# Second feed-forward product of a hybrid layer as one level of Strassen's scheme, on one Trainium2 core

## The chip, the cores and the metric

One core of a Trainium2 chip runs the whole kernel. TensorE (PE) does matrix products, VectorE (DVE) and ScalarE (ACT) elementwise work, GpSimd (POOL) a little set-up, and SyncE (SP) issues most DMAs. The metric is the device time of one execution in microseconds, the median of several.

## The reference

One layer of a model with 512 tokens (L), width 1024 (D) and a feed-forward width of 4096 (FF); everything is fp32. After a mixing part with attention comes the end that matters here:

```python
merged = jax.nn.sigmoid(gate_a) * ya + jax.nn.sigmoid(gate_b) * yb
y = merged @ w_out[l]
x = x + ga1 * rmsnorm(y, g_post_mix[l])

h = rmsnorm(x, g_pre_ffn[l]) * (1.0 + sc2) + sh2
u = jax.nn.relu(h @ w_ff1[l])
y = (u * u) @ w_ff2[l]
x = x + ga2 * rmsnorm(y, g_post_ffn[l])
```

Here ya and yb are the outputs of the two mixers times their `up` weights, gate_b is made late as h times the `gate` weights, and ga1, sc2, sh2 and ga2 are columns of silu(c) @ w_ada.

## The kernel before

Every fp32 product is made of three matmuls in a reduced fp32 format: an operand is split into a high half (a copy rounded to that format, on ScalarE, L109) and a low half (the difference, on VectorE, L110), and high x high, high x low and low x high are added up in PSUM (mm3, L137 through mm). A weight block of 128 x 1024 (512 KB) comes by `stage` (L103 to L106): one DMA on SyncE's queue into one of three buffers of the ring `st`, handed out in program order. `wload` (L115 to L125) splits it into `whi` and `wlo`, four buffers each, and a fifth where the list `wmore` names a pool.

The stages in order: attention with the first projections; the merge stage (L629 to L676), which for each of eight column blocks m has 24 matmuls of a `gate` block (on `hTh`, `hTl`, into `mm`) and 24 of an `up` block (on `obh`, `oah` and their low halves, into `s`), and some columns of the product of `ada` with silu(c), made on VectorE (L210) from `in_ada_dram` blocks in the same ring; the product with `w_out` (L704 to L783), with the norm of each token tile behind it, which leaves `h2h` and `h2l`; the first feed-forward product (L786 to L813); the second (L814 to L846).

silu_rows (L154 to L160) makes silu(c) as rows: a DMA `cb` of c to all 128 partitions, a sigmoid into `sg` (tile name `cs`), and a product. It is called twice, at the merge stage and in front of the first feed-forward product. The vector products that follow in each stage read `cb`.

The first feed-forward product takes its first four weights (EARLY) in two halves, tiles 0 and 1 and then tiles 2 and 3. Work on the engines is put in order by a scheduler from the program and its dependencies; buffers of a ring are taken in program order.

The second product goes over 32 blocks k of the 4096 rows. For each it splits u[k] (uh, ul) and the weight block, and for four token tiles t adds 3 x 2 matmuls of 128 x 512 into eight PSUM banks (accs): 768 matmuls. The last four blocks (LAST) are taken tile by tile, so that the norm, gate and store of one tile (residual) run beside the matmuls of the next.

Of the kernel before, what the change touches and what calls it, by code (L numbers as in the profile page):

```python
# [14 lines left out]
P = 128  # L15
# [23 lines left out]
LAST = 4  # L39
# [22 lines left out]
def layer_kernel(tc, x, ada, vecs, c_row, rope, w_first, w_v, w_b, w_a, w_gate, w_up, w_out, w_ff1, w_ff2, out):  # L62
    nc = tc.nc
    es = ExitStack()
    with es:
# [631 lines left out]
        wmore.append(x1p)  # L697
# [92 lines left out]
        silu_rows(f2p)  # L790

        def ff1(m, w, t0, t1):
# [21 lines left out]
        accs = [[bank(a), bank(b)] for a, b in (("tr", "tr"), ("mm", "mm"), ("s", "s"), ("s", "o"))]  # L814

        def ff2(t, k, uw, ns):
            (uh, ul), (hi, lo) = uw
            ts = slice(t * P, (t + 1) * P)
            f, l = k == 0, k == MF - 1
            for s, w, first, last in ((uh, hi, f, False), (uh, lo, False, False), (ul, hi, False, l)):  # L820
                for n in ns:
                    mm(accs[t][n], s[:, ts], w[:, n * 512:(n + 1) * 512], first, last)

        def operands(k):
            w = wload(w_ff2[k])
            uh = f2p.tile([P, L], F32R, name=uid("uh"), tag="uh", bufs=5)
            ul = f2p.tile([P, L], F32R, name=uid("ul"), tag="ul", bufs=5)
            split(uh, ul, u2[k])
            return (uh, ul), w
# [5 lines left out]
        uws = [operands(k) for k in range(MF - LAST, MF)]  # L835
        ov = out.rearrange("(t p) d -> t p d", p=P)
        for t in range(NT):
            for n in range(2):
                for i in range(LAST):
                    ff2(t, MF - LAST + i, uws[i], (n,))  # L840
# [78 lines left out]
```

## Time and profile before

| | us |
|---|---|
| median of 3 runs | 811.65 (811.42 to 813.32) |
| profiled execution | 811.92 |
| its span | 810.1 |
| TensorE busy | 786.3 (97%) |
| VectorE busy | 511.0 (63%) |
| ScalarE busy | 363.0 (45%) |
| attention ends (last `o` matmul) | 324.55 |
| first `w_ff1` matmul | 452.20 |
| first and last matmul of the second product | 629.5, 803.6 |

The profile is one execution, recorded by the hardware; times in it are microseconds from the start of its span. Engines run at the same time, so that only work on the chain that ends last counts. Matmuls overlap one another in the engine: one of 512 columns is listed with some 389 ns, while they start 0.227 us apart. The times of DMA issues are when SyncE's queue gave them out; a DMA lands some microseconds later.

### The profile page before, as it was taken

How to read it: one execution, taken by the hardware profiler on the slowest of the kernel's cores; microseconds unless marked ns; L12 is line 12 of the kernel's file. 1: busy time of each engine (PE TensorE's matmuls, PEld its weight loads, DVE VectorE, ACT ScalarE, POOL GpSimd, SP SyncE). 2: the span in 40 equal slices, each digit the busy share in tenths (PEclk: the TensorE clock that was granted, in tenths of full speed). 3: DMA queues.
4: the chain of work that ended last, by engine and by line, in shares of the span. 5: the costliest groups of instructions: out<-in, count | busy, mean ns of one | idle time of the engine just before them, and what ended most of it. 6: DMA issues, size and time to landing. Idle time of an engine off the chain costs nothing.

```text
span 810.1 us, 10809 instructions
## 1 busy us (share of the span) xinstructions
PE 786.3 (97%) x4110; PEld 656.4 (81%) x4110; DVE 511.0 (63%) x973; ACT 363.0 (45%) x684; POOL 2.8 (0%) x15
## 2 busy tenths in 40 slices
PE   6999999989999999999999999999999999999996
PEld 5889977658889887887688998888888888888885
DVE  6876799999956776788767863344433433333325
ACT  6555657464546677631347753223322322332322
POOL 0000000000000000000000000000000000000000
PEclk9999999999999999999999999999999999999999
DMA  9933201122121210578780332344442232233202
GB/s 356 377 117 104 78 27 53 56 75 79 60 98 53 79 53 27 163 264 256 248 315 28 123 127 89 131 138 137 141 156 99 83 105 89 93 104 104 79 1 104
DMA packets 27987, 98.58 MB, mean 122 GB/s; under 512 B 3360, under 2 KB 3360, under 8 KB 27936
## 3 DMA queue, kind: packets, MB, share of 16 engines
q1 hardware_dynamic: 27216, 96.82, 35.2%
q10 hardware_dynamic: 720, 1.08, 0.4%
q8 instruction: 32, 0.52, 0.3%
q14 instruction: 19, 0.16, 0.1%
HBM read 95.79 MB, written 2.10 MB: 121 GB/s over the span
## 4 chain that ended last, share of the span: by engine, by line
PE 76%; DVE 15%; DMA 6%; issue 2%; ACT 2%; DVEq 0%; SPq 0%; ACTq 0%
PE mm L137 30%; PE s L137 27%; PE o L137 9%; PE tr L137 7%; DMA st<-in_ada_dram 3%; DVE a L483 3%; DVE isc L409 2%; DVE sm L408 2%; DVE wlo L110 2%; DMA st<-in_w_up_dram 2%; PE tr L427 1%; DVE be L485 1%; DVE st L210 1%; PE tr L333 1%; DVE qT L521 1%
## 5 line engine op out<-in xcount | busy, mean ns | idle before, releaser
L109 ACT ACTIVATE whi<-st 128x1024 fp32r<-128x1024 f32 (+2 forms) x122 | 127.5, 1047 | 180.8 <-PE mm L137 45.3
L110 DVE TENSOR_TENSOR wlo<-st,whi 128x1024 fp32r<-128x1024 f32 (+2 forms) x122 | 147.1, 1209 | 92.2 <-ACT whi L109 91.9
L137 PE MATMUL mm<-hTh,whi 128*128 128x512 f32 x192 | 78.7, 410 | 0.1
L110 DVE TENSOR_TENSOR ul<-u,uh 128x512 fp32r<-128x512 f32 x32 | 22.2, 692 | 89.7 <-ACT uh L109 89.6
L137 PE MATMUL mm<-hTh,wlo 128*128 128x512 f32 x192 | 75.6, 394 | 0.0
L137 PE MATMUL mm<-hTl,whi 128*128 128x512 f32 x192 | 75.4, 393 | 0.0
L109 ACT ACTIVATE uh<-u 128x512 fp32r<-128x512 f32 x32 | 20.2, 631 | 108.7 <-PE o L137 105.1
L137 PE MATMUL mm<-whi,hTh 128*128 128x256 f32 (+2 forms) x208 | 62.3, 306 | 0.1
L137 PE MATMUL mm<-whi,hTl 128*128 128x256 f32 (+2 forms) x208 | 60.2, 296 | 0.0
L137 PE MATMUL mm<-wlo,hTh 128*128 128x256 f32 (+2 forms) x208 | 60.1, 295 | 0.0
L210 DVE CUSTOM_DVE_ANT_0 st<-st,cb,vec 128x1024 f32<-128x1024 f32 x32 | 40.9, 1282 | 29.1 <-DMA st<-in_ada_dram 29.0
L137 PE MATMUL s<-h2h,whi 128*128 128x512 f32 (+1 forms) x144 | 52.7, 366 | 0.0
L137 PE MATMUL s<-h2l,whi 128*128 128x512 f32 (+1 forms) x144 | 52.6, 366 | 0.0
L137 PE MATMUL s<-h2h,wlo 128*128 128x512 f32 (+1 forms) x144 | 52.6, 366 | 0.0
L137 PEld LDWEIGHTS mm<-hTh,wlo 128*128 128x128 f32 x192 | 36.3, 189 | 7.8
L137 PEld LDWEIGHTS mm<-hTh,whi 128*128 128x128 f32 x192 | 36.5, 190 | 6.6 <-DVE qT L521 0.3
L137 PEld LDWEIGHTS mm<-hTl,whi 128*128 128x128 f32 x192 | 36.5, 190 | 6.2
L137 PEld LDWEIGHTS mm<-wlo,hTh 128*128 128x128 f32 x208 | 39.5, 190 | 1.0
L137 PEld LDWEIGHTS mm<-whi,hTl 128*128 128x128 f32 x208 | 39.5, 190 | 0.6
L137 PEld LDWEIGHTS mm<-whi,hTh 128*128 128x128 f32 x208 | 39.0, 190 | 0.7 <-ACT ka L544 0.3
L137 PE MATMUL mm<-h2h,wlo 128*128 128x512 f32 (+1 forms) x96 | 35.7, 372 | 0.0
L137 PE MATMUL mm<-h2h,whi 128*128 128x512 f32 (+1 forms) x96 | 35.7, 371 | 0.0
(296 smaller groups left out, 1755.1 us busy)
## 6 DMA issues: line engine op xcount, KB each, us to landing
st<-in_w_ff_dram SPq DMA_DIRECT2D x64, 512.0 KB, 3.3
st<-in_ada_dram SPq DMA_DIRECT2D x32, 512.0 KB, 4.2
sa<-in_ada_dram SPq DMA_DIRECT2D x16, 512.0 KB, 8.1
st<-in_w_gate_dram SPq DMA_DIRECT2D x16, 512.0 KB, 3.3
st<-in_w_first_dram SPq DMA_DIRECT2D x8, 512.0 KB, 8.5
st<-in_w_b_dram SPq DMA_DIRECT2D x8, 512.0 KB, 3.3
st<-in_w_a_dram SPq DMA_DIRECT2D x8, 512.0 KB, 3.2
st<-in_w_up_dram SPq DMA_DIRECT2D x8, 512.0 KB, 4.3
```

The costliest lines, as they stand in the source:

```text
L109: nc.scalar.activation(dst_hi, src, AF.Copy)
L110: nc.vector.tensor_tensor(dst_lo, src, dst_hi.bitcast(F32), op=ALU.subtract)
L137: nc.tensor.matmul(o, lhsT, rhs, start=start, stop=stop)
L210: nc.vector.tensor_tensor_reduce(out=st, in0=st, in1=cb[0], scale=1.0, scalar=vec[:, j:j + 1], op0=ALU.mult, op1=ALU.add, accum_out=mod[:, ...
L333: nc.tensor.transpose(ps[:, t * P:(t + 1) * P], s[:, t, i:i + 2].rearrange("p a d -> p (a d)"), identr)
L408: nc.vector.max(out=m8, in_=cur)
L409: nc.vector.match_replace(out=cur, in_to_replace=m8, in_values=cur, imm_value=SENT)
L427: nc.tensor.transpose(tr[:, j * P:(j + 1) * P], ps[e][:, j * P:(j + 1) * P], ident)
L483: nc.vector.tensor_tensor_scan(a[:, n - 1::-1], a[:, n - 1::-1], zero.to_broadcast([P, n]), 1.0, op0=ALU.mult, op1=ALU.add)
L485: nc.vector.tensor_tensor(be[:, :n - 1], be[:, :n - 1], a[:, 1:n], op=ALU.mult)
L521: nc.vector.scalar_tensor_tensor(qq[o, e], ps[r], QK_SCALE, qq[r, e].bitcast(F32), op0=ALU.mult, op1=ALU.subtract)
```

## The change

The second feed-forward product becomes one level of Strassen's scheme in the form with seven products: the tokens, the 4096 rows and the 1024 output columns are each cut in two halves. Blocks of u are paired (p = 0 to 15, two blocks of 128 rows). A first pass over the pairs makes four of the seven block products (p1, p5, p6, p7), each a half of the tokens by a half of the columns, 24 matmuls of 512 columns a step; then their sums are formed in PSUM and SBUF (u2, c22, v7), and a second pass adds the three others (18 matmuls a step) onto p1, p5 and p7. The sums of u (token_sums) are made behind the first product, the sums of weights in front of each step: the right halves of both weight blocks of a pair come as a new argument, w_right, and from step 2 on the difference to the block that was loaded is made by a DMA of GpSimd that adds w_right onto the negated copy (column_sums). In this part the order on TensorE, VectorE and ScalarE is written out by hand (manual_schedule). LAST is 3.

Two more edits stand in the diff. silu_rows takes `sg` from the ring `st` in place of its own tile, and the fifth weight buffer (wmore) is dropped.

```diff
...
-LAST = 4
+LAST = 3
+NP = MF // 2
+HB = L // 2
+A11, S1, S3, S2, A12, A22 = range(6)
...
         def silu_rows(pool):
             dst = pool.tile([P, D], F32, name=uid("cb"), tag="cb")
-            sg = pool.tile([P, D], F32, name=uid("cs"), tag="cs")
+            sg = per.tile([P, D], F32, name=uid("cs"), tag="st", bufs=3)
             nc.sync.dma_start(dst, c_row.to_broadcast([P, D]))
             nc.scalar.activation(sg, dst, AF.Sigmoid)
             nc.vector.tensor_tensor(dst, dst, sg, op=ALU.mult)
...
-        wmore.append(x1p)
...
-        u2 = [u2p.tile([P, L], F32, name=f"u2_{m}") for m in range(MF)]
+
+        def block_tile(name, dt):
+            return u2p.tile([P, 6 * HB], dt, name=uid(name), tag="ub", bufs=NP)
+
+        blocks = [block_tile("ub", F32) for p in range(NP)]
         f2p = es.enter_context(tc.tile_pool(name="f2p", bufs=1, side="right"))
         ga2b = f2p.tile([P, D], F32, name="ga2b")
         silu_rows(f2p)
...
+            u = blk(m // 2, 4 * (m % 2), 2)[:, cs]
+            nc.scalar.activation(u, ps[:, cs], AF.Relu)
+            nc.vector.tensor_tensor(u, u, u, op=ALU.mult)
+
+        def token_sums(p):
+            nc.vector.tensor_tensor(blk(p, S3), blk(p, A11), blk(p, S1), op=ALU.subtract)
+            nc.vector.tensor_tensor(blk(p, S1), blk(p, S1), blk(p, A22), op=ALU.add)
+            nc.vector.tensor_tensor(blk(p, S2), blk(p, S1), blk(p, A11), op=ALU.subtract)
...
         for m in range(EARLY, MF):
             ff1(m, wload(w_ff1[m]), 0, NT)
-            if m % 2 and m >= MF - 2 * KT:
-                i = (m - MF + 2 * KT) // 2
-                ada_cols(40 + i)
-                gated_gain(KT + i, 40 + i, 72 + i)
+            if m % 2:
+                token_sums(m // 2)
+                if m >= MF - 2 * KT:
+                    i = (m - MF + 2 * KT) // 2
+                    ada_cols(40 + i)
+                    gated_gain(KT + i, 40 + i, 72 + i)
         rows_of(ga2b, ga[:, KT:], evac)
...
-        for k in range(MF - LAST):
-            uw = operands(k)
-            for t in range(NT):
-                ff2(t, k, uw, (0, 1))
...
+        p1, p6, p5, p7 = [[bank(a), bank(b)] for a, b in (("tr", "tr"), ("s", "o"), ("s", "s"), ("mm", "mm"))]
...
+        def load(j):
+            xw[j] = stage(w_ff2[2 * j]) if j < NP else stage(w_ff2[2 * (j - NP) + 1])
+
+        def column_sums(p):
+            nw[p] = ntile().bitcast(F32)
+            nc.scalar.activation(nw[p], xw[p], AF.Copy, scale=-1.0)
+            nc.gpsimd.dma_start(nw[p], w_right[p], accum_op=ALU.add)
+
+        def first_ops(p):
+            a = pair_tile(p, "ah")
+            x, n = xw[p], nw[p]
+            (h1, l1), (h2, l2) = wtile(), wtile()
+            t2 = blk(p, 0, 2)
+            if p != 1:
+                split(a[:, 0], a[:, 1], blk(p, 0, 4))
+            split(h1[:, H0], l1[:, H0], x[:, H0])
+            if p < 2:
+                nc.vector.tensor_tensor(n, n, x, op=ALU.subtract)
+            if p == 1:
+                split(h2, l2, n)
+                split(a[:, 0], a[:, 1], blk(p, 0, 4))
+            nc.vector.tensor_tensor(t2, n[:, H1], x[:, H0], op=ALU.add)
+            if p != 1:
+                split(h2, l2, n)
+            split(h1[:, H1], l1[:, H1], t2)
+            nc.vector.tensor_tensor(blk(p, S2), blk(p, A12), blk(p, S2), op=ALU.subtract)
+            firsts[p] = (a[:, 0], a[:, 1]), (h1, l1), (h2, l2)
+
+        def first_products(p):
+            a, w1, w2 = firsts.pop(p)
+            order = [(p1, A11, w1, H0), (p5, S1, w2, H0), (p7, S3, w2, H1), (p6, S2, w1, H1)]
+            if p in (0, NP - 1):
+                order = [order[i] for i in ((0, 1, 3, 2) if p == 0 else (0, 3, 1, 2))]
+            for acc, b, w, cs in order:
+                for i in range(2):
+                    product(acc, i, a, b * HB, w, cs, p == 0, p == NP - 1)
...
+        def second_ops(p):
+            if p:
+                a = block_tile("a2", F32R)
+                ah, al = a[:, :3 * HB], a[:, 3 * HB:]
+            else:
+                a = pair_tile(0, "ah")
+                ah, al = a[:, 0, :3 * HB], a[:, 1, :3 * HB]
+            y, n, w = xw[NP + p], ntile(), wtile()
+            t2 = blk(p, 0, 2)
+            split(w[0], w[1], y)
+            nc.vector.tensor_tensor(t2, y[:, H0], t2, op=ALU.subtract)
+            split(ah, al, blk(p, 3, 3))
+            split(n[:, H0], n[:, H1], t2)
+            seconds[p] = (ah, al), w, (n[:, H0], n[:, H1])
...
+        on_p1, on_p5, on_p7 = (p1, 1, 1, H0), (p5, 0, 1, H1), (p7, 2, 2, H0)
+
+        for j in range(2):
+            load(j)
+            if j == 0:
+                nw[0] = stage(w_right[0])
+        first_ops(0)
+        nw[1] = stage(w_right[1])
+        load(2)
+        for p in range(NP):
+            if p + 1 < NP:
+                first_ops(p + 1)
+                if p == 0:
+                    load(3)
+                    column_sums(2)
+            if p == NP - 1:
+                second_ops(0)
+            load(p + 4)
+            if p + 3 < NP:
+                column_sums(p + 3)
+            first_products(p)
+        u2 = f3p.tile([P, 2, 512], F32, name="u2")
+        c22 = f3p.tile([P, 2, 512], F32, name="c22")
+        v7 = f2p.tile([P, D], F32, name="v7", tag="cb")
+        for i in range(2):
+            nc.scalar.activation(u2[:, i], p1[i], AF.Copy)
+        for i in range(2):
+            nc.vector.tensor_tensor(u2[:, i], p6[i], u2[:, i], op=ALU.add)
+        for i in range(2):
+            nc.scalar.activation(c22[:, i], p5[i], AF.Copy)
+        for i in range(2):
+            nc.scalar.activation(v7[:, i * 512:(i + 1) * 512], p7[i], AF.Copy)
+        second_ops(1)
+        for p in range(NP - LAST):
+            load(NP + p + 4) if p + 4 < NP else None
+            second_ops(p + 2)
+            for args in (on_p1, on_p5, on_p7):
+                for i in range(2):
+                    second_product(*args, p, i)
...
```

The diff leaves out the operands of each step (first_ops, second_ops make the splits that the program's matmuls read), the change-over between the passes, and the new loop over the last steps, which takes the tiles in the order 2, 3, 0, 1. In both kernels the names of a tile in the following rows end in numbers that the program gives out; lines of the changed kernel stand two or three later. The rows of the trace write `in_w_ff_dram` for the weights of both feed-forward products.

SyncE's queue at the end of the attention, before. `st` from `in_w_up_dram`, `in_w_gate_dram` and `in_ada_dram` are the merge stage's weights, `cb` is silu_rows' first load:

```order
L105 DMA st_618_3199<-in_w_gate_dram 128x1024
L105 DMA st_733_3628<-in_w_up_dram 128x1024
L105 DMA st_737_3660<-in_w_gate_dram 128x1024
L105 DMA st_742_3698<-in_w_up_dram 128x1024
L105 DMA st_746_3730<-in_w_gate_dram 128x1024
L105 DMA st_751_3768<-in_ada_dram 128x1024
L105 DMA st_752_3772<-in_ada_dram 128x1024
L105 DMA st_753_3776<-in_ada_dram 128x1024
L157 DMA cb_730_3620<-in_c_row_dram 128x1024
L105 DMA st_754_3780<-in_w_up_dram 128x1024
```

The same stretch of SyncE's queue in the changed kernel:

```order
L108 DMA st_618_3199<-in_w_gate_dram 128x1024
L160 DMA cb_730_3620<-in_c_row_dram 128x1024
L108 DMA st_733_3628<-in_w_up_dram 128x1024
L108 DMA st_737_3660<-in_w_gate_dram 128x1024
L108 DMA st_742_3698<-in_w_up_dram 128x1024
L108 DMA st_746_3730<-in_w_gate_dram 128x1024
L108 DMA st_751_3768<-in_ada_dram 128x1024
L108 DMA st_752_3772<-in_ada_dram 128x1024
L108 DMA st_753_3776<-in_ada_dram 128x1024
L108 DMA st_754_3780<-in_w_up_dram 128x1024
```

`cb` moved from behind seven weight loads to a place ahead of them. On TensorE the blocks that use the first of these weights stood, in part, ahead of the attention's last matmuls (`o`); before:

```order
L137 MATMUL s_741_3667<-obh_727_3609,wlo_735_3631 128x512
L137 MATMUL s_740_3666<-oah_589_3085,whi_734_3630 128x512
L427 MATMUL tr_724_3570<-identr_69,p_720_3548 128x128 x4
L137 MATMUL o_725_3577<-pT_680_3432,va_79_589 64x512
L137 MATMUL o_725_3577<-pT_681_3433,va_79_589 64x512
L137 MATMUL o_725_3577<-pT_680_3432,va_79_589 64x384
```

and in the changed kernel the last four of the attention are followed by the first of the `up` block:

```order
L140 MATMUL o_725_3577<-pT_681_3433,va_79_589 64x256
L140 MATMUL o_725_3577<-pT_680_3432,va_79_589 64x128
L140 MATMUL o_725_3577<-pT_681_3433,va_79_589 64x128
L140 MATMUL s_741_3667<-obh_726_3608,whi_734_3630 128x512
L140 MATMUL s_741_3667<-obl_728_3610,whi_734_3630 128x512
```

Thirteen matmuls of that `up` block and thirteen of a `gate` block stood ahead of the last `o` matmul; all 26 stand behind it now.

SyncE's queue at the start of the first feed-forward product, before:

```order
L717 DMA x1_3_4284<-in_x_dram 128x1024
L105 DMA st_914_4802<-in_w_ff1_dram 128x1024
L105 DMA st_917_4808<-in_w_ff1_dram 128x1024
L105 DMA st_920_4814<-in_w_ff1_dram 128x1024
L105 DMA st_923_4820<-in_w_ff1_dram 128x1024
L105 DMA st_934_5042<-in_w_ff1_dram 128x1024
L105 DMA st_938_5075<-in_w_ff1_dram 128x1024
L105 DMA st_942_5108<-in_w_ff1_dram 128x1024
L105 DMA st_946_5141<-in_w_ff1_dram 128x1024
L157 DMA cb_912_4797<-in_c_row_dram 128x1024
L105 DMA st_950_5174<-in_w_ff1_dram 128x1024
```

and in the changed kernel:

```order
L108 DMA st_843_4342<-in_w_out_dram 128x1024
L160 DMA cb_928_4781<-in_c_row_dram 128x1024
L108 DMA st_930_4786<-in_w_ff1_dram 128x1024
L108 DMA st_933_4792<-in_w_ff1_dram 128x1024
L108 DMA st_936_4798<-in_w_ff1_dram 128x1024
```

`cb` stood behind eight `w_ff1` loads and now stands ahead of the first.

## Rows read from the trace of the kernel before

**Rows 1.** The page, part 1: busy time (share of the span) x instructions.

```profile
PE 786.3 (97%) x4110; PEld 656.4 (81%) x4110; DVE 511.0 (63%) x973; ACT 363.0 (45%) x684; POOL 2.8 (0%) x15
```

**Rows 2.** Stretches: width, then PE, PEld, DVE, ACT, POOL busy, clock, DMA share, GB/s.

```profile
6.00:8.00 2.00, 0.04 (x1) 0.07 (x1) 0.98 (x3) 1.94 (x6) 0.00 (x0) 1.00 1.00 395
330.00:405.00 75.00, 72.14 (x312) 57.66 (x312) 62.30 (x102) 23.01 (x31) 0.00 (x0) 1.00 0.76 244
629.00:804.00 175.00, 175.00 (x775) 144.44 (x773) 64.36 (x78) 50.88 (x74) 0.00 (x0) 1.00 0.25 85
806.00:808.00 2.00, 0.00 (x0) 0.00 (x0) 1.04 (x2) 0.00 (x0) 0.00 (x0) 0.76 0.36 139
808.00:810.00 2.00, 0.00 (x0) 0.00 (x0) 0.00 (x0) 0.00 (x0) 0.00 (x0) 0.50 0.32 123
```

**Rows 3.** Matmuls by form, 620 to 810: count, ns min/median/max, first to last start.

```profile
L137 PE MATMUL mm<-whi,uh x64: 387/389/474, 629.5 to 792.3; 128*128 128x512 f32 x64
...
L137 PE MATMUL o<-whi,uh x32: 389/389/389, 634.1 to 803.2; 128*128 128x512 f32 x32
```

**Rows 4.** The chain of waits, 324 to 405: shares by engine and line.

```profile
by line: DMA st<-in_ada_dram 28.4%; DMA st<-in_w_up_dram 16.2%; PE s L137 13.3%; DVE st L210 12.3%; DVE wlo L110 7.5%; DMA st<-in_w_gate_dram 5.5%; ACT whi L109 5.3%; issue 3.7%; PE mm L137 3.1%; DVE mrg L662 1.7%; PE o L137 0.9%; DVE mrg L
```

**Rows 5.** SyncE's issues around the attention's end: start, us, what.

```profile
253.41 0.33 SPq L105 DMA_DIRECT2D st<-in_w_up_dram  x1
...
324.62 0.33 SPq L157 DMA_DIRECT2D cb<-in_c_row_dram  x1
332.48 0.33 SPq L105 DMA_DIRECT2D st<-in_w_up_dram  x1
```

**Rows 6.** SyncE's issues at the start of the first feed-forward product.

```profile
416.66 41.52 SPq L105 DMA_DIRECT2D st<-in_w_ff_dram  x8
463.69 0.33 SPq L157 DMA_DIRECT2D cb<-in_c_row_dram  x1
```

**Rows 7.** Groups by form, 629.4 to 804: count, busy us, mean ns, idle before.

```profile
L110 DVE TENSOR_TENSOR wlo<-st,whi 128x1024 fp32r<-128x1024 f32 x28 | 34.3, 1225 | 6.9 <-ACT whi L109 6.9
...
L109 ACT ACTIVATE whi<-st 128x1024 fp32r<-128x1024 f32 x28 | 29.2, 1044 | 3.9 <-PE mm L137 3.9
...
L110 DVE TENSOR_TENSOR ul<-u,uh 128x512 fp32r<-128x512 f32 x27 | 18.7, 693 | 88.2 <-ACT uh L109 88.2
L109 ACT ACTIVATE uh<-u 128x512 fp32r<-128x512 f32 x27 | 17.1, 632 | 105.1 <-PE o L137 105.1
```

**Rows 8.** The page, part 6: DMA issues, count, KB, median us to landing.

```profile
st<-in_w_ff_dram SPq DMA_DIRECT2D x64, 512.0 KB, 3.3
...
st<-in_w_first_dram SPq DMA_DIRECT2D x8, 512.0 KB, 8.5
```

**Rows 9.** Timeline around the attention's end: start, us, what.

```profile
321.46 3.09 PE L137 MATMUL o<-pT,va 128*64 128x512 f32 x16
...
324.58 0.60 ACT L109 ACTIVATE oah<-o 128x512 fp32r<-128x512 f32 x1 [2.15 <-PE o L137]
...
325.20 1.28 ACT L664 ACT_TABLE_LOAD   x1
...
326.49 1.95 ACT L664 ACTIVATE sga<-sga,mz 128x512 f32<-128x512 f32 x3
...
329.59 0.39 PE L137 MATMUL s<-obh,whi 128*128 128x512 f32 x1
```

**Rows 10.** Timeline around the first matmuls of the first feed-forward product.

```profile
452.20 0.36 PE L137 MATMUL s<-h2h,whi 128*128 128x256 f32 x1
...
459.12 1.06 PE L756 MATMUL tr<-identr,xn 128*128 128x128 f32 x8
...
462.32 1.29 DVE L110 TENSOR_TENSOR h2l<-h2f,h2h 128x512 fp32r<-128x512 f32 x2 [0.26 <-ACT h2h L109]
```

**Rows 11.** Tile `cb`: its sigmoid (ns min/median/max), and its transfer.

```profile
L158 ACT ACTIVATE cs<-cb x2: 1044/1053/1062, 328.4 to 467.5; 128x1024 f32<-128x1024 f32 x2
...
DMA to landing us min/median/max: 3.5/3.6/3.7
```

More of the change, by code (lines that the diff above doesn't have):

```diff
@@ L59, with layer_kernel @@
 EDGE = 224
-def layer_kernel(tc, x, ada, vecs, c_row, rope, w_first, w_v, w_b, w_a, w_gate, w_up, w_out, w_ff1, w_ff2, out):
+def layer_kernel(tc, x, ada, vecs, c_row, rope, w_first, w_v, w_b, w_a, w_gate, w_up, w_out, w_ff1, w_ff2, w_right, out):
     nc = tc.nc
@@ L790, in layer_kernel, with blk @@
         silu_rows(f2p)
+        def blk(p, a, n=1):
+            return blocks[p][:, a * HB:(a + n) * HB]
         def ff1(m, w, t0, t1):
@@ L816, in ff2 @@
[L816 to L829, printed above, removed]
@@ new lines, in layer_kernel, with pair_tile @@
+        rows_of(ga2b, ga[:, KT:], evac)
+        h2_es.close()
+        f3p = es.enter_context(tc.tile_pool(name="f3p", bufs=1))
+        m_es = ExitStack()
+        m_es.enter_context(tc.manual_schedule(engines={mybir.EngineType.DVE, mybir.EngineType.Activation, mybir.EngineType.PE}))
+        p1, p6, p5, p7 = [[bank(a), bank(b)] for a, b in (("tr", "tr"), ("s", "o"), ("s", "s"), ("mm", "mm"))]
+        H0, H1 = slice(0, 512), slice(512, D)
+        def pair_tile(p, name):
+            return (f2p, f3p)[p % 2].tile([P, 2, D], F32R, name=uid(name), tag="ah")
@@ new lines, in wtile, with ntile, product @@
+        def wtile():
+            return [per.tile([P, D], F32R, name=uid(n), tag=n, bufs=WBUF) for n in ("whi", "wlo")]
+        def ntile():
+            return f3p.tile([P, D], F32R, name=uid("wn"), tag="wn", bufs=3)
+        def product(acc, i, a, c0, w, cs, first, last, onto=False):
+            (ah, al), (hi, lo) = a, w
+            ts = slice(c0 + i * P, c0 + (i + 1) * P)
+            for s, m, f, l in ((ah, hi, first, False), (ah, lo, False, False), (al, hi, False, last)):
+                nc.tensor.matmul(acc[i], s[:, ts], m[:, cs], start=f, stop=l, skip_group_check=onto)
@@ new lines, in layer_kernel, with half_done @@
+        second_ops(NP - 1)
+        ov = out.rearrange("(t p) d -> t p d", p=P)
+        jk = f3p.tile([P, 512], BF16, name="jk2")
+        def half_done(t, n, yg, y, whole):
+            cs = slice(n * 512, (n + 1) * 512)
+            ss = small()
+            if not whole:
+                nc.vector.tensor_tensor(yg[:, cs], y, u2[:, t % 2], op=ALU.add)
+                y = yg[:, cs]
+            nc.scalar.activation(jk, y, AF.Square, accum_out=ss)
+            nc.vector.tensor_tensor(yg[:, cs], y, ga2b[:, cs], op=ALU.mult)
+            return ss
@@ new lines, in layer_kernel @@
+        for t in (2, 3, 0, 1):
+            i = t % 2
+            yg = pair_tile(t, "yg")[:, 0].bitcast(F32)
+            if t >= 2:
+                s1 = partial(half_done(t, 1, yg, c22[:, i], True))
+                for p in range(NP - LAST, NP):
+                    second_product(*on_p7, p, i)
+                s2 = half_done(t, 0, yg, p7[i], False)
+            else:
+                for p in range(NP - LAST, NP):
+                    second_product(*on_p5, p, i)
+                s1 = partial(half_done(t, 1, yg, p5[i], False))
+                for p in range(NP - LAST, NP):
+                    second_product(*on_p1, p, i)
+                s2 = half_done(t, 0, yg, p1[i], True)
+            r = rstd_of(s2, s1)
@@ L838, in layer_kernel @@
             for n in range(2):
-                for i in range(LAST):
-                    ff2(t, MF - LAST + i, uws[i], (n,))
-            def store(n, cs):
+                cs = slice(n * 512, (n + 1) * 512)
+                nc.vector.scalar_tensor_tensor(x1[t][:, cs], yg[:, cs], r, x1[t][:, cs], op0=ALU.mult, op1=ALU.add)
                 (nc.sync, nc.scalar)[n].dma_start(ov[t][:, cs], x1[t][:, cs])
-            residual(f2p, accs[t], x1[t], ga2b, store)
-        h2_es.close()
+        m_es.close()
```

16 lines of the change are left out of this document (11 added, 5 removed).

## The prediction

> **What bounds the kernel now.** I read the busy shares and then the chain first: TensorE works 97% of the span [rows 1], so a second counts only where TensorE has work less, or is kept from it. The table of stretches shows that the second feed-forward product is TensorE work from end to end: 175.00 us busy of 175.00 [rows 2]. The list of its matmuls by form [rows 3] has twelve forms for the product, four accumulator names by three operand pairs; two of them are shown. They come to 768 matmuls of 512 columns, from 629.5 to 803.2 and so 0.2268 us each (the 389 ns of one row overlap those of its neighbours). The one place where TensorE is not the bound is the merge stage, which the chain of waits from 324 to 405 gives to DMAs and what hangs on them: 28.4% on the loads of the `ada` weights and 16.2% on `w_up`, TensorE's `s` matmuls only 13.3% [rows 4]. All these loads stand on one queue, SyncE's, which issues in order; so I read that queue's timeline last [rows 5, 6], and it decides my forecast.
>
> **The arithmetic that goes.** The scheme needs 16 steps of 24 matmuls and 16 of 18: 672 in place of 768. The 96 that go are worth 96 x 0.2268 = 21.8 us [rows 3].
>
> **What the scheme adds inside the product.** Durations of elementwise work by size [rows 7]: ScalarE 1.04 (1024 columns) and 0.63 (512), VectorE 1.23 and 0.69; for 256 columns I estimate 0.4. In the first pass a step gives VectorE two instructions of 1024, three of 512 and one of 256, 2 x 1.23 + 3 x 0.69 + 0.4 = 4.9 us, ScalarE three of 1024 (the negation for the weight difference is one) and two of 512, 4.4 us, TensorE 24 x 0.2268 = 5.44 us. The order is fixed by hand, and the two engines hand to each other: a_hi, a_lo, h1's low half, t2, h1's second half and the negation in a row are 1.04 + 1.23 + 0.69 + 0.69 + 0.63 + 1.04 = 5.3 us, with semaphore hops about 5.5, equal to TensorE's step. So TensorE stays the bound or loses some hundredths of a microsecond per step: between 0 and 16 x 0.3 = 5, I take 1. The second pass gives VectorE 3.6 and ScalarE 2.5 us against 18 x 0.2268 = 4.08: no loss. The three sums per pair of token tiles in the first feed-forward product are about 1.2 us of VectorE in some 11 us, beside matmuls that own their stretch: nothing.
> The accumulating transfer of the weight difference is in no row. From step 3 on it has almost two steps, about 10 us, before the add that needs it. The nearest rows are a plain 512 KB load, 3.3 us alone and 8.5 us in the crowded start [rows 8]; both fit. For step 2 it is not hidden: its negation stands behind step 1's whole exchange, so it starts about 6.5 us into the product and is wanted at about 8.4; between 0 and 6 us of stall, I take 2 (nearer to the 3.3 row). At the change of passes ScalarE drains six banks ahead of the next operands: 1.5. Sum inside the product: +4.5, with ends 0 and 13.
>
> **What moves, and costs more than it looks.** The change also puts `sg` of silu_rows into the three-buffer ring `st`, whose tiles are handed out in program order. The order on SyncE shows it: `cb`, which stood behind seven weight loads in the merge stage and behind eight of `w_ff1` at the next stage, now stands ahead of all of them. And `cb` waits: for the last `o` matmul of the attention (it starts at 324.62, the `o` group ends at 321.46 + 3.09 = 324.55 [rows 5, 9]), and the second time for the last low half of h2 (463.69, behind 462.32 + 1.29 = 463.61 [rows 6, 10]). Nothing in SyncE's queue passes it.
>
> *Merge stage.* The seven loads went out from 253.41 on, over 50 us before the attention ended [rows 5]; now they follow its end. With them 26 matmuls (13 of `gate`, 13 of `up`; 26 x 0.2268 = 5.9 us) and four weight splits (4 x 1.04 on ScalarE, 4 x 1.23 on VectorE) leave the attention's tail, which ends earlier for it: by at most 5.9, by 1 if the softmax on ScalarE and VectorE bounds it; I take 2.5, so T = 322.0. From T: `cb` lands at +3.8 (3.5 to 3.7 measured [rows 11]), ScalarE meanwhile has 0.60 + 1.28 (table) + 1.95 (three sigmoids) [rows 9], `cs` +5.0, four more sigmoids +7.5, whi of the first `up` +8.6, wlo +9.9. TensorE then has 24 matmuls of `up` and 24 of `gate`, 10.9 us, to +20.8: 342.8, at a point that it passed at 329.59 [rows 9], 13.2 late. What is left of the stage, 7 blocks of `up` and 6 of `gate`, is 312 matmuls or 70.8 us, to 413.6; before, the stage took 75.5 from there, since the DMA chain held it. That chain starts later too: the load `up2` that went out at 332.48 [rows 5] waits for the first `ada` product with `cb`, whose weight gets its ring buffer only from the split of the `gate` block (+12.2), then lands (4.4, since 3.3 alone) and is multiplied (1.3): T + 17.9 = 339.9, +7.4. Before, it carried the stage to 405.1, so now to some 412.5. I take +8.5, the later of the two; ends 5 (tail gains all 5.9) and 11.
>
> *Start of the first feed-forward product.* Four of the eight `w_ff1` loads were issued from 416.66 on and all within 41.5 us [rows 6], so that matmuls on tiles 0 and 1 ran from 452.20 [rows 10] while tiles 2 and 3 were still being normalised. Now the first load goes out behind `cb`, at the end of the norm chain, which itself isn't changed: 463.7 in old time. `cb` lands +3.7 (467.4; three transfers share the engines, so maybe +1), table load 1.28, `cs` 1.05 [rows 9, 11], whi 1.04, wlo 1.23 with hops: 471.9. TensorE starts there in place of 452.2, 19.7 late, less 1.0 for the transposes of tile 3 that used to stand inside this stretch [rows 10]: 18.7. I take 18.8; ends 16 and 21. The weights behind it follow one another in time (each half block is 24 x 0.12 = 2.9 us), and from there on the stage is TensorE's, as before.
>
> **The clock.** The granted clock falls from 1.00 to 0.76 in 806 to 808 and 0.50, the 1.2 GHz level, in 808 to 810, after TensorE's last matmul near 804 [rows 2]. So idle stretches of some 10 and 18 us can let it fall; how long matmuls then run at half speed is in no row. Bounds: 0, and 6 us, if all 48 matmuls of the first two half blocks (5.8 us) take twice as long; I take 1.
> The Trainium skill ("TensorE: Matmul & The Clock Gate", "What's actually happening") says that the array is throttled by default and that activity releases it; by its figures an estimate is 1.7 us lost for each return from idle, 3.4 for two, and the sum would be 825. The fall at the end of this trace agrees; the start does not, where TensorE is busy 0.04 of 2 us and is still granted 1.00 [rows 2].
>
> **The sum.** The profiled execution took 811.9 us, 0.3 above the median of 811.65. 811.9 - 21.8 + 4.5 + 8.5 + 18.8 + 1.0 = 822.9; for the median 822.6. The end of the kernel, last matmul to last store, has the same two halves and stays.
>
> **Rivals.**
> *The queue does not hold the weights (faster).* If `cb` is released early, because its memory in the new layout has another last user, the first product starts as before. Then 811.7 - 21.8 + 4.5 + 8.5 = 802.9 with the merge loss, 794.4 without it. It decides as soon as both losses together fall under 15 us. For it: `cb`'s place in memory is the allocator's. Against it: in both places the trace has `cb` within 0.1 us of the event it waits for [rows 5, 6, 9, 10], and the second one lies in a pool that opens at the same point of the program. I give 0.11.
> *Losses that just cancel:* tail gain 5.9, FF1 loss 16, no stall in the product: 811.7 - 21.8 + 5 + 16 = 810.9. All of these at once: 0.05.
> *The accumulating transfer paces the first pass (much slower).* Two of them can be in flight. If one takes X from issue to landing and 2 us go to negation and hops, a step takes (X + 2) / 2; over 5.44 that counts from X = 9 on. X = 12.5, one and a half times the slowest 512 KB row, gives 7.25, 14 x 1.8 = +25 and 848. For it: no row shows this kind of transfer, and GpSimd issues only 15 instructions in this kernel. Against it: DMA in the product moves 85 GB/s [rows 2], the new one some 190 in the first pass, against 244 that the trace held for whole stages. 0.10.
> *Forecast, slower for the queue:* 0.74; its own range is 816 to 831 (stalls 0 to 9, merge 5 to 11, start 17 to 20, clock 0 to 3).
>
> **How the numbers follow.** 0.3%, 2.4 us, is about what a measurement of this kernel can tell from no change. Faster 0.11; same 0.05; slower 0.74 + 0.10 = 0.84. The range 811 to 836 leaves out the faster rival and most of the transfer rival.
>
> **What would show it.** Right: SyncE issues `cb` directly behind the last `o` and the last h2 low half, with `w_up` and `w_ff1` behind it; TensorE idle some 8 to 10 us after the attention and some 18 before the first `w_ff1` matmul; a product of about 157 us. Wrong: `w_ff1` loads issued before 450; a product over 165 us with VectorE waiting for `wn` in each step; a merge stage that ends where it did. If the idle stretches are there and the time is still under 811, I have mis-sized the product.

## The result, and the profile after

The changed kernel takes 839.87 us (median; 836.66 to 840.34), the kernel before 812.49 beside it: ratio 1.0326, interval 1.0292 to 1.036. Slower, as forecast, but by 27.4 us where 10.9 were forecast, and outside the range. The profiled execution has a span of 837.9 us against 810.1.

Where the 27.8 us of span arose, from the same events in both traces (positive: lost):

| stretch | before | after | lost | forecast |
|---|---|---|---|---|
| start to the attention's end (`cb` issued) | 324.62 | 327.88 | +3.3 | -2.5 |
| from there to the second `cb` (merge, `w_out`, norm) | 139.07 | 152.27 | +13.2 | +11.0 |
| from there to the product's first matmul | 165.77 | 187.20 | +21.4 | +18.8 |
| the product, first to last matmul's start | 174.17 | 158.78 | -15.4 | -17.3 |
| from there to the end of the span | 6.47 | 11.77 | +5.3 | 0 |
| (clock, not placed) | | | | +1 |

SyncE's issues of the changed kernel, the rows that answer to [rows 5, 6] (start, us, what):

```profile
252.30 0.33 SPq L108 DMA_DIRECT2D st<-in_w_gate_dram  x1
327.88 0.33 SPq L160 DMA_DIRECT2D cb<-in_c_row_dram  x1
328.26 0.42 SPq L108 DMA_DIRECT2D st<-in_w_up_dram  x1
...
480.15 0.33 SPq L160 DMA_DIRECT2D cb<-in_c_row_dram  x1
480.59 15.89 SPq L108 DMA_DIRECT2D st<-in_w_ff_dram  x7
```

The queue does what the forecast said: `w_up` follows `cb`, 75 us later than before, and no `w_ff1` load goes out before 480. But the queue is only part of it. Two of the seven loads go out right behind `cb` (328.26 and 328.74); the third goes out only when the product that reads `cs` is done, 333.20 + 1.23 = 334.43:

```profile
333.20 1.23 DVE L162 TENSOR_TENSOR cb<-cb,cs 128x1024 f32<-128x1024 f32 x1 [4.05 <-ACT cs L161]
334.46 0.33 SPq L108 DMA_DIRECT2D st<-in_w_up_dram  x1
```

So `sg` (tile `cs`) also holds one of the ring's three buffers until `cb` has landed and been multiplied. No run puts `cb` on another queue; what the order on the queue costs without the held buffer is not shown.

What the forecast did not have is in the table of stretches of the changed kernel (columns as in [rows 2]):

```profile
306.00:316.00 10.00, 9.19 (x53) 6.04 (x51) 7.27 (x30) 9.69 (x25) 0.00 (x0) 1.00 0.00 0
316.00:324.00 8.00, 5.71 (x19) 2.45 (x21) 3.09 (x11) 3.60 (x10) 0.00 (x0) 0.65 0.01 2
324.00:328.00 4.00, 3.80 (x14) 2.00 (x10) 0.06 (x1) 0.16 (x1) 0.00 (x0) 0.50 0.00 0
328.00:338.00 10.00, 1.33 (x3) 0.62 (x3) 3.14 (x3) 9.54 (x13) 0.00 (x0) 0.50 0.64 210
338.00:342.00 4.00, 4.00 (x10) 3.17 (x11) 2.36 (x2) 1.90 (x3) 0.00 (x0) 0.50 0.68 199
342.00:421.00 79.00, 79.00 (x350) 65.40 (x349) 64.81 (x107) 22.36 (x29) 0.00 (x0) 1.00 0.79 256
...
480.00:489.00 9.00, 0.80 (x2) 0.50 (x2) 2.27 (x3) 4.23 (x4) 0.00 (x0) 0.50 0.49 176
```

The clock column (third from the right) falls to 0.50, the 1.2 GHz level, inside the attention's tail, before TensorE has stood idle for long: the 26 matmuls that stood there before are gone behind `cb`, and TensorE is busy 5.71 of 8 us. It stays low through the wait and beyond TensorE's return. The timeline of that return:

```profile
336.62 0.79 PE L140 MATMUL s<-obh,whi 128*128 128x512 f32 x1 [8.82 <-ACT whi L112]
...
338.48 0.63 PE L140 MATMUL s<-obh,whi 128*128 128x512 f32 x1
338.90 0.63 PE L140 MATMUL s<-obl,whi 128*128 128x512 f32 x1
...
345.27 0.39 PE L140 MATMUL mm<-hTl,whi 128*128 128x512 f32 x1
345.50 0.39 PE L140 MATMUL mm<-hTh,wlo 128*128 128x512 f32 x1
```

Matmuls start 0.42 us apart at 338, 0.23 at 345. Twelve of them, from 336.62 to 341.89, run at the low level: 12 x (0.42 - 0.23), some 2.3 us at most, since the first three also wait for their splits. At the start of the first feed-forward product the same happens:

```profile
484.42 1.28 ACT L161 ACT_TABLE_LOAD   x1 [5.09 <-DMA cb<-in_c_row_dram]
...
487.77 0.58 PE L140 MATMUL s<-h2h,whi 128*128 128x256 f32 x1 [10.98 <-ACT whi L112]
...
489.60 0.41 PE L140 MATMUL s<-h2h,whi 128*128 128x256 f32 x1
489.81 0.41 PE L140 MATMUL s<-h2l,whi 128*128 128x256 f32 x1
```

Two matmuls of 256 columns are 0.21 us apart, and 16 run at this level. Before, they were 0.12 apart:

```profile
452.64 0.28 PE L137 MATMUL s<-h2h,whi 128*128 128x256 f32 x1
452.76 0.28 PE L137 MATMUL s<-h2l,whi 128*128 128x256 f32 x1
```

In the product, the accumulating transfers (tile `wn`, as the view of that tile gives them) are no bound:

```profile
L865 POOL DMA_DIRECT2D wn<-in_w_right_dram x14: 862/862/1011, 673.9 to 742.8; - x14
...
DMA to landing us min/median/max: 5.2/5.4/7.9
```

Between the two ends that I had from plain loads, 3.3 and 8.5 [rows 8]. From 686 to 752 TensorE is busy 66.00 of 66.00 us. It waits only around step 2 and once ahead of the last loop. The end is another matter. The timeline from the last matmuls:

```profile
825.99 0.68 DVE L966 TENSOR_TENSOR yg<-s,u 128x512 f32<-128x512 f32 x1
...
826.13 0.39 PE L855 MATMUL tr<-whi,a 128*128 128x512 f32 x1
826.71 0.63 ACT L968 ACTIVATE jk<-yg 128x512 bf16<-128x512 f32 x1 [2.56 <-DVE yg L966]
...
830.31 0.68 DVE L966 TENSOR_TENSOR yg<-s,u 128x512 f32<-128x512 f32 x1
...
833.30 1.42 DVE L990 SCALAR_TENSOR_TENSOR x<-yg,sm,x 128x512 f32<-128x512 f32 x2
```

When TensorE finishes, VectorE is only at the first sum (`yg<-s,u`) of the last tile but one; the last tile follows 4.3 us later. In the kernel before, only the second half of one tile and its last operations were left behind the last matmul:

```profile
803.63 0.39 PE L137 MATMUL o<-whi,ul 128*128 128x512 f32 x1
...
805.63 1.41 DVE L692 SCALAR_TENSOR_TENSOR x<-yg,sm,x 128x512 f32<-128x512 f32 x2
```

### The profile page after: what moved, and what is told of

It reads as the page before. It is cut to its first block, busy times and chain, and to the rows that moved or that the text cites. A ratio compares the mean times of both kernels' runs of the same rounds, so it can differ in the third digit from the quotient of the medians.

```text
span 837.9 us, 10847 instructions
## 1 busy us (share of the span) xinstructions
PE 775.4 (93%) x4014; PEld 644.2 (77%) x4014; DVE 601.9 (72%) x1127; ACT 417.4 (50%) x752; POOL 15.0 (2%) x29
## 4 chain that ended last, share of the span: by engine, by line
PE 69%; DVE 19%; ACT 7%; DMA 2%; issue 2%; ACTq 0%; DVEq 0%; SPq 0%
PE mm L140 27%; PE s L140 22%; PE o L140 6%; DVE wlo L113 4%; PE s L855 3%; DVE a L486 2%; PE mm L855 2%; DVE isc L412 2%; DVE sm L411 2%; PE tr L855 2%; ACT whi L112 2%; DVE be L488 1%; PE tr L430 1%; PE tr L140 1%; PE tr L336 1%
## 5 line engine op out<-in xcount | busy, mean ns | idle before, releaser
L113 DVE TENSOR_TENSOR wlo<-st,whi 128x1024 fp32r<-128x1024 f32 (+3 forms) x124 | 141.0, 1140 | 90.3 <-ACT whi L112 90.2
L112 ACT ACTIVATE whi<-st 128x1024 fp32r<-128x1024 f32 (+3 forms) x124 | 122.7, 992 | 151.4 <-PE s L140 51.1
L140 PEld LDWEIGHTS s<-h2h,whi 128*128 128x128 f32 x144 | 27.9, 194 | 15.7 <-ACT whi L112 11.4
L855 PE MATMUL s<-whi,ah 128*128 128x512 f32 x100 | 36.0, 389 | 0.0
L140 PE MATMUL mm<-h2l,whi 128*128 128x512 f32 (+1 forms) x96 | 35.7, 371 | 0.0
```

Of the source, the lines that this page charges most:

```text
L112: nc.scalar.activation(dst_hi, src, AF.Copy)
L113: nc.vector.tensor_tensor(dst_lo, src, dst_hi.bitcast(F32), op=ALU.subtract)
L140: nc.tensor.matmul(o, lhsT, rhs, start=start, stop=stop)
L855: nc.tensor.matmul(acc[i], s[:, ts], m[:, cs], start=f, stop=l, skip_group_check=onto)
```

## The experiments

Theory: the line in silu_rows costs all that is lost ahead of the product, by the loads that it holds and by the clock; the scheme itself gains less than its matmuls, through its end. Rivals: other edits (the fifth buffer, the layout) carry part of the loss; the accumulating transfer holds the product; the clock's fall is a matter of one profile.

**own_tile, before_ring: the line alone, taken out and put in.** The first is the changed kernel with the left part of this, the second the kernel before with one line:

```diff
 own_tile                                               before_ring
-sg = per.tile(..., tag="st", bufs=3)                  -sg = pool.tile(..., tag="cs")
+sg = pool.tile(..., tag="cs")   # second call: ga2b   +sg = per.tile(..., tag="st", bufs=3)
```

Expected of own_tile: 

> The changed kernel with the sigmoid of silu_rows out of the ring st: a tile of its own in the first call, the still unused ga2b in the second. Theory (queue): everything lost ahead of the second product comes from cb standing ahead of the weight loads. Up to the end of the first feed-forward product the changed kernel lost 36.8 us (629.2 to 666.0), so this kernel takes 839.9 - 36.8 = 803 us (801 to 805), its first w_ff1 matmul is back near 452, and its second product and end still take 5 us longer at the end than before. Rival (other edits: the fifth weight buffer that went, the new layout of u): part of the loss stays, 810 or more, and the first w_ff1 matmul stays later than 458.

Expected of before_ring: 

> The kernel before with one line of the change: sg of silu_rows taken from the ring st. Theory (queue): this line alone costs the whole loss, 812.0 + 36.8 = 849 (846 to 852), with cb issued at about 328 and 480 and TensorE's granted clock at 0.5 in the attention's tail. Rival (other edits): under 840. Rival (my prediction's sizes, 8.5 + 18.8 + 1): 840.

Measured: own_tile 805.34 us, ratio to before 0.9912 (0.9892 to 0.9932); before_ring 847.32, ratio 1.043 (1.0408 to 1.0452). So the line costs 839.87 - 805.34 = 34.5 us in the one kernel and 847.32 - 812.52 = 34.8 in the other. This is shown from both sides: with the line out, the change is faster than the kernel before. One part of the expectation of before_ring did not come: in its profile the clock holds through the tail (1.00 to 326, then 0.55), and `cb` goes out at 323.37 and 475.30, not at 328 and 480. SyncE of own_tile:

```profile
325.54 0.33 SPq L161 DMA_DIRECT2D cb<-in_c_row_dram  x1
...
418.29 42.46 SPq L108 DMA_DIRECT2D st<-in_w_ff_dram  x7
466.26 0.33 SPq L161 DMA_DIRECT2D cb<-in_c_row_dram  x1
```

**first_own, second_own: one call each** (single runs).

```diff
-silu_rows(mp)     # first_own: sg of the first call in a tile of its own
+silu_rows(mp, True)
-silu_rows(f2p)    # second_own: sg of the second call in ga2b
+silu_rows(f2p, ga2b)
```

Expected of first_own: 

> The changed kernel, sg in a tile of its own in the first call only (merge stage). Theory (queue, two separate losses): saves the 16.4 us lost between the attention's tail and the merge stage's end: 839.9 - 16.4 = 823.5; the start of the first feed-forward product still loses 20.4. Rival (the two overlap, the second takes over what the first gives back): 830 or more.

Expected of second_own: 

> The changed kernel, sg out of the ring in the second call only. Theory (queue, two separate losses): saves the 20.4 us at the start of the first feed-forward product: 819.5. Rival (overlap): 830 or more.

Measured: 826.95 and 816.52, each some 3 us off its theory and under the 830 of the rival. Against own_tile the second call's wait costs 21.6 us and the first call's 11.2. Both losses stand by themselves; the sum, 32.8, is 1.7 under the 34.5, which single runs do not settle. What they do show is the clock: second_own has the same order on TensorE as the changed kernel up to the attention's end, yet its clock holds to about 326:

```profile
318.00:320.00 2.00, 1.43 (x6) 0.61 (x6) 0.00 (x0) 1.27 (x3) 0.00 (x0) 1.00 0.03 8
...
322.00:324.00 2.00, 1.25 (x9) 0.65 (x5) 0.14 (x2) 0.70 (x2) 0.00 (x0) 1.00 0.00 0
...
326.00:328.00 2.00, 0.00 (x0) 0.00 (x0) 0.00 (x0) 1.51 (x3) 0.00 (x0) 0.50 0.97 352
```

SyncE of second_own, then the group of the last `o` matmuls of 512 columns (308 to 330) in the changed kernel and in second_own, where one takes 618 ns in place of 853:

```profile
251.53 0.33 SPq L108 DMA_DIRECT2D st<-in_w_gate_dram  x1
323.33 0.33 SPq L161 DMA_DIRECT2D cb<-in_c_row_dram  x1
```

```profile
L140 PE MATMUL o<-pT,va 128*64 128x512 f32 x8 | 6.1, 853 | 1.2 <-DVE pT L187 0.7 <-ACT pT L185 0.6
```

```profile
L140 PE MATMUL o<-pT,va 128*64 128x512 f32 x8 | 4.3, 618 | 1.3 <-DVE pT L188 0.7 <-ACT pT L186 0.6
```

The attention ends 4.55 us earlier than in the changed kernel (323.33 against 327.88). Of this, 0.77 stood between the two profiles at the `gate` load (251.53 against 252.30), before any of it; the other 3.8 us are what the fall of the clock cost in the tail.

**fill_after: is it the clock?** The changed kernel plus matmuls that nobody reads:

```diff
+fill = bank("mm")
+for j in range(26):
+    mm(fill, hTh[j % KT][:, :P], hTl[j % KT], j == 0, j == 25)
```

Expected: 

> The changed kernel with 26 matmuls of 512 columns added in the attention's tail whose result nobody reads; the order puts them ahead of the tail and a real gate block into it. Theory (clock): in the changed kernel's profile the granted clock falls to 0.5 at 318, and the attention ends at 327.9 and not near 323.3, where it ends in second_own with the same order on TensorE and the clock at 1.00 until 325; with TensorE kept busy the clock stays at 1.00 to the end of the attention, which ends by 325, and the time is 839.9 - 3 = 837 (835 to 838). Rival (the matmuls just cost their 5.9 us, since TensorE is the bound before the tail): 841 or more. Rival (the fall at 318 is a matter of one profile): 840 with the clock at 1.00.

Measured: 832.83 us, 7.0 under the changed kernel, ratio to before 1.025 (1.0231 to 1.0268). Work without use makes it faster, by more than I expected; the rival that the matmuls just cost their 5.9 us falls. The attention ends at 321.1, 6.8 earlier than in the changed kernel, with the clock at 1.00:

```profile
316.00:318.00 2.00, 2.00 (x14) 1.31 (x13) 0.41 (x2) 1.36 (x3) 0.00 (x0) 1.00 0.03 8
...
322.00:324.00 2.00, 1.53 (x7) 0.94 (x5) 0.39 (x1) 1.99 (x3) 0.00 (x0) 1.00 0.97 225
```

The 7.0 us are not the clock's alone. Of the 6.8, 1.5 stood in the profile before the tail (the `gate` load goes out at 250.78 here, at 252.30 there), and 3.8 is what second_own shows for the clock. The rest, 1.5, is open, since the edit also changes the order: the filler stands at 296 to 313, and the last real `gate` block, which ended at 306.8 in the changed kernel, now stands at 313 to 323, among and behind the last `o` matmuls. From the first `cb` to the second both profiles take the same (152.6 and 152.3 us).

Against the rival that the fall is a matter of one profile stand the runs' mean clocks: three runs of the changed kernel have 0.967 (839.81 to 840.34 us) and one 0.972 (836.66); before_ring has 0.977 twice (845.33, 845.93) and 0.972 and 0.970 (848.72, 848.91). So one program's runs differ by some 3 us with the clock, near the 3.8. Where in those runs it fell is not recorded.

**before_4buf: the fifth buffer.** The kernel before without `wmore.append(x1p)`. Expected: 

> The kernel before without the fifth weight buffer (the line wmore.append(x1p) taken out), nothing else. In own_tile the first w_ff1 matmul starts at 454.8, in the kernel before at 452.2, and the second product 3.3 us later. Theory (the fifth buffer let work of the next stage stand ahead of time): 812.8 + 2.5 = 815 (814 to 816.5). Rival (the 2 to 3 us come from elsewhere, run to run or the new layout): 812 to 813.

Measured: 813.27 us, ratio 1.0014 (1.0001 to 1.0027). The fifth buffer is worth about 1 us, too little to carry the loss.

**staged: no accumulating DMA.** On own_tile:

```diff
-nc.scalar.activation(nw[p], xw[p], AF.Copy, scale=-1.0)
-nc.gpsimd.dma_start(nw[p], w_right[p], accum_op=ALU.add)
+nc.sync.dma_start(nw[p], w_right[p])
-if p < 2:
-    nc.vector.tensor_tensor(n, n, x, op=ALU.subtract)
+nc.vector.tensor_tensor(n, n, x, op=ALU.subtract)
```

Expected: 

> As own_tile, without the accumulating DMA: every w_right block is loaded plainly by SyncE and subtracted on VectorE (1.22 us more there per first-pass step, 1.04 less on ScalarE). Theory (the accumulating transfer is hidden from step 3 on and earns the VectorE time): VectorE's 4.93 + 1.22 = 6.15 us per step becomes the bound against TensorE's 5.44, +0.7 in 13 steps, less 3 for the stall at step 2: 805.3 + 6 = 811 (808 to 815). Rival (the accumulating transfer is what holds the first pass back): 803 or less.

Measured: 810.99 us, ratio 0.9978 (0.9966 to 0.9991), as the theory had it: its first pass has TensorE busy 54.91 of 60 us (660 to 720), where own_tile has 60.00. The transfer earns some 5.6 us. That it paces the pass, my rival, is refuted.

**early2, start_store: the wait at step 2.** early2 moves `column_sums(2)` ahead of `first_ops(1)` in own_tile; start_store also moves `column_sums(3)` behind `first_ops(2)`, and has the stores of sp_store (below).

Expected of early2: 

> As own_tile, with the negation and the accumulating transfer of step 2 issued ahead of step 1's operands in place of behind them. Theory (late start): in own_tile TensorE idles 2.7 us around step 2 and its clock then falls to 0.5 from 648.9 to 654.8, some 2.9 us more; started about 3 us earlier, the transfer is there in time: 805.3 - 4 = 801 (799.5 to 803). Rival (the transfer is slow because DMA is full there, share 1.0 from 644 to 648): under 1 us gained, 804.5 or more. Rival (the negation now delays step 1's operands by its 1.06 us): step 1 waits instead, 805 to 807.

Expected of start_store: 

> As sp_store, with step 2's negation and transfer ahead of step 1's operands and step 3's negation behind step 2's operands. Theory (ScalarE's order makes the wait at step 2, the transfer itself is in time): TensorE's idle time from 640 to 650 falls from about 3 us to under 1.5 and the clock stays at 1.00: sp_store less 2 to 4. Rival (the operands of step 2 need ScalarE and VectorE longer than TensorE's step anyway): as sp_store within 1 us.

Measured: early2 804.42, ratio 0.9899 (0.9881 to 0.9917), above the range expected and not apart from own_tile's. The transfer was in time, and ScalarE waited for something else, a load ahead of step 3's negation, which stands ahead of step 2's operands on its queue (timeline of early2):

```profile
642.20 1.06 ACT L865 ACTIVATE wn<-st 128x1024 f32<-128x1024 f32 x1 [2.74 <-DMA st<-in_w_ff_dram]
...
643.16 1.04 ACT L112 ACTIVATE ah<-ub 128x1024 fp32r<-128x1024 f32 x1
```

start_store: 806.54, ratio 0.9919 (0.9899 to 0.9938). The wait moved one step on, TensorE idles 3.3 us between 650 and 660. Both repairs hand the wait on to another operand in ScalarE's order; I did not find the one that ends it.

**The end: tail_early, bound, tail2, sp_store, best, best2.** All on own_tile. tail_early gives GpSimd the subtraction of each second-pass step and the sums into c22, and finishes two column halves early:

```diff
-nc.vector.tensor_tensor(t2, y[:, H0], t2, op=ALU.subtract)
+nc.gpsimd.tensor_tensor(t2, y[:, H0], t2, op=ALU.subtract)
```

Expected: 

> As own_tile, with less VectorE work from the change of passes to the end: the subtraction of each second-pass step and the two sums into c22 go to GpSimd, and the column halves of tiles 2 and 3 that are complete after step 3 (square sum on ScalarE, gain on VectorE) are done at steps 8 and 10 in place of the last loop. Theory (the end is bound by VectorE, 5.2 us longer than before, and by its late second-pass operands, 1.45 us): 805.3 - 5 = 800 (798.5 to 802), last matmul to end 7 to 8 us in place of 11.4. Rival (the end is a chain of latencies between ScalarE and VectorE, the amount of VectorE work does not matter): 1 to 2 us gained, 803.5 or more. Rival (GpSimd is slow at it and the chain waits for it): slower than 805.

Measured: 806.40 us, ratio 0.9919 (0.9891 to 0.9946), no gain. The time alone fits both rivals. The profile speaks for the slow GpSimd: the end did get shorter, 10.4 us from the last matmul's start (795.0 to 805.4) where own_tile has 11.8, while TensorE waits 2.5 us for VectorE's `a` behind the change of passes. GpSimd's operations, and VectorE's under them (groups by form, then the timeline: `a<-ub,a` of 768 columns once beside a GpSimd operation, once alone; the median of 15 is 2.05):

```profile
L907 POOL TENSOR_TENSOR ub<-st,ub 128x512 f32<-128x512 f32 x16 | 26.7, 1667 | 36.1 <-DMA st<-in_w_ff_dram 36.1
```

```profile
776.22 2.05 DVE L113 TENSOR_TENSOR a<-ub,a 128x768 fp32r<-128x768 f32 x1
...
779.93 0.95 DVE L113 TENSOR_TENSOR a<-ub,a 128x768 fp32r<-128x768 f32 x1
```

bound puts `second_ops(1)` ahead of the copies at the change of passes. Expected: 

> As own_tile, with the operands of the second pass's step 1 put ahead of the copies out of PSUM at the change of passes (program order on ScalarE and VectorE). Theory (VectorE begins the second pass late and stays behind: it works 3.56 us per step against TensorE's 4.08 and still makes TensorE wait 1.4 us before the last loop): the wait before the last loop goes, the tail stays: 805.3 - 1.5 = 804 (803 to 805). Rival (the copies then hold up TensorE at the change of passes by as much): 805 to 807.

Measured: 803.92, ratio 0.9906 (0.9872 to 0.9939). The wait ahead of the last loop went, and 1.2 us of waiting came at the change of passes (8.77 busy of 10 from 720 to 730): no gain that parts from own_tile.

tail2 has bound's edit, the two halves early, a scratch tile for the sums, and a tile's last operations behind the next tile's first. best is tail2 with early2's edit. Expected of tail2: 

> As bound, with another end and nothing on GpSimd: the complete column halves of tiles 2 and 3 are finished at steps 8 and 10, sums go to a scratch tile so that the gain product does not wait for ScalarE's square of the same tile, and a tile's last operations stand behind the next tile's first in VectorE's order. Theory (the end is VectorE waiting for ScalarE in its own order, some 5 us of waits from own_tile's 785 to 802): last matmul to end 7.0 us in place of 11.4, 805.3 - 1.5 - 4.4 = 799.5 (798 to 801). Rival (the end is bound by the amount of VectorE work): 803 or more.

Expected of best: 

> tail2 with early2's edit (step 2's accumulating transfer ahead of step 1's operands), which gave 0.9 us in the median and 4 in the profile: 798.5 (796.5 to 800.5). Rival (step 1 then waits for what step 2 gains): as tail2.

Measured: 806.32, ratio 0.9923 (0.9895 to 0.9951), and 806.98, ratio 0.993 (0.9904 to 0.9955): a miss both, with 12.0 us from the last matmul's start to the end where 7.0 were expected. In own_tile's timeline I then read this wait:

```profile
788.80 0.34 ACTq L992 DMA_DIRECT2D out_dram<-x  x1
...
789.19 0.63 ACT L969 ACTIVATE jk<-c 128x512 bf16<-128x512 f32 x1 [2.07 <-DVE x L991]
```

ScalarE's square of the next tile stands behind its own issue of a store, which waits for VectorE. sp_store takes only that away:

```diff
-(nc.sync, nc.scalar)[n].dma_start(ov[t][:, cs], x1[t][:, cs])
+nc.sync.dma_start(ov[t][:, cs], x1[t][:, cs])
```

Expected: 

> As own_tile, with all output stores issued by SyncE in place of every second one by ScalarE. Theory (ScalarE's queue: a store that waits for VectorE holds the next tile's square): the waits of ScalarE for VectorE's x (2.07 us in each of three tiles) go, last matmul to end 8 us in place of 11.4: 805.0 - 3.4 = 801.6 (800.5 to 803). Rival (VectorE's own order and amount bind): the waits become waits elsewhere, 804 or more.

Measured: 803.81, ratio 0.9888 (0.9868 to 0.9909), the lowest ratio of the study, though not apart from own_tile's. From the last matmul's start to the end it is 11.05 us (789.15 to 800.2), where 8 were expected: ScalarE's waits behind its stores went, and the end is still longer than expected: VectorE's own order binds. Its timeline has the last two tiles' sums 4.3 us apart as before, with VectorE waiting for ScalarE's square inside each:

```profile
788.35 0.68 DVE L967 TENSOR_TENSOR yg<-s,u 128x512 f32<-128x512 f32 x1
...
789.82 0.69 DVE L970 TENSOR_TENSOR yg<-yg,ga2b 128x512 f32<-128x512 f32 x1 [0.79 <-ACT jk L969]
...
792.67 0.68 DVE L967 TENSOR_TENSOR yg<-s,u 128x512 f32<-128x512 f32 x1
```

best2 is start_store with tail2's end. Expected: 

> start_store with tail2's end (operands of step 1 ahead of the change of passes, two halves finished early, sums into a scratch tile, last operations behind the next tile's first). Theory: without the stores on ScalarE the shorter VectorE chain shows, last matmul to end 7 us: 1 to 3 us under start_store, 796 to 799. Rival (VectorE still waits for ScalarE's square, which reads the same PSUM bank): as start_store.

Measured: 807.18, ratio 0.9924 (0.9907 to 0.9941), a miss. The end falls to 9.4 us (795.9 to 805.3), so the shorter chain shows there, and 3.7 us of a new wait at step 3 with a fall of the clock behind it takes it back.

Across these kernels, staged (177.8) left out, the time from the product's first matmul to the end of the span is 170.4 (early2) to 174.5 us (tail_early), against 180.6 before. The changed kernel itself has 170.5: none of my repairs got clearly below it. And the same program ahead of the product starts it at 632.7 in own_tile's profile and 629.2 in sp_store's: differences of 1 to 3 us between these kernels are not settled by one profile.

## Why the prediction was wrong

Right: the direction, the line that costs, and its two places. The order on SyncE, read before any run, named the line that costs 34.5 us; `cb` went out directly behind the last `o` matmul and the last h2 low half; the accumulating transfer was hidden from step 3 on, and the two rivals that it paces the pass, and that the queue doesn't hold the weights, fell. Staged's 811 came out as its step time said.

Wrong were sizes, all on one side, 16.8 us of span together:

- **"I take 2.5, so T = 322.0"**: the attention ended at 327.9, 5.8 later. The step counted the 26 matmuls and the splits as work taken away, and not as what kept TensorE busy and its clock up. The fall of the clock in the tail cost 3.8; 0.9 stood in the profile before the tail (the `gate` load at 252.30, before at 251.40); and the gain itself was 1.4 in place of 2.5 (second_own, where the clock held, counted from the same load).
- **"The clock ... I take 1"**: I had bounds of 0 and 6, took 1 without a reason, and let the clock act only on matmuls after the two idle stretches. By the rows above it cost 3.8 in the tail, up to 2.3 at the merge stage's start (12 matmuls at 0.42 in place of 0.23) and 1.5 at the first feed-forward product (16 matmuls at 0.21 in place of 0.12): some 7.6 us. That the clock would fall inside the tail, while TensorE still worked 1.2 of every 2 us, I did not consider. The Trainium skill's estimate that stood beside it ("TensorE: Matmul & The Clock Gate", "What's actually happening"), 3.4 us for two returns, is near what those two cost (3.8) and has nothing for the tail.
- **"The end of the kernel ... has the same two halves and stays"**: it grew by 5.3 us. The step looked at which halves there are and not at how fast TensorE brings them. Before, a tile of the last loop had 24 matmuls (5.4 us); now 9 or 18 (2.0 and 4.1), and VectorE's and ScalarE's 4.3 us per tile became the bound there. It was the largest term that I had set to nothing without a sum. That VectorE's order is the cause is read from the rows; no repair brought the end back to the 6.5 us of before.
- **Waits inside the product (4.5 taken)** came to 158.8 - 672 x 0.2268 = 6.4 us, and 8.7 in own_tile, where the wait at step 2 also lets the clock fall (0.75 in 650 to 660).
- **The two queue terms** were good: 8.5 for the merge stage against 11.2 measured by itself, of which up to 2.3 is the clock at the return; 18.8 for the start against 21.6, of which 1.5 is the clock. Both measurements are single runs.

Three slips in the working carry no weight: 471.9 adds up to 472.0 before any hops; 0.2268 us per matmul follows from the last start at 803.63, not from the 803.2 beside it; and the three sums are per pair of 128-row blocks of u, not of token tiles.

So the forecast split was 28.3 us lost by the line and 17.3 gained by the scheme; measured, 34.5 lost and 7.2 gained (812.52 to 805.34).

## What to carry to other kernels

A buffer's ring is also a place in a queue: moving a scratch tile of 512 KB into the ring that feeds the weights put a late wait ahead of seven and of eight loads, and the order of the issuing engine shows it before any run. The tile also holds one of the ring's buffers until its own late input has come. When a loop's matmuls are cut by an eighth, sum the other engines' work per tile again where the last loop runs, since the engine that was covered before becomes the bound there. Matmuls that fill a latency-bound stretch can be part of its speed; when they are moved out, let the range hold the stretch at half the clock. Here that was 3.8 us, and it came in one of three profiles with the same order of work.

## What the runs showed of the hardware that I had not expected

Twenty-six matmuls of no use made the kernel 7.0 us faster (832.83 against 839.87). In its profile the clock held at 1.00 through a tail in which it had fallen to 0.50 with TensorE busy about two thirds of the time; how much of the 7.0 is the clock, and how much the order of work that changed with them, is not separated. With the same order of work the fall came at 318 in one profile (the changed kernel) and at 326, behind the tail, in two others (second_own, before_ring). An elementwise operation of 512 columns took GpSimd 1.67 us in the mean (VectorE 0.69), and a VectorE operation beside one took 2.05 in place of 0.95. An accumulating DMA of 512 KB landed in 5.2 to 7.9 us (a plain one 3.3 in the same stretch) and occupied GpSimd's queue for 0.86.
